# Two decoder layers on one core: the seven-product units of the down-projection reordered, with their sums in x's room, none in a layer's last pass, and the convolution released two pieces later

## The chip, the core and the metric

The kernel is one launch on one core of a Trainium2 chip. The metric is the device time of that launch in microseconds, lower is better. Three runs of the kernel before took 2187.38, 2190.59 and 2194.48 us, so the median is 2190.59 us.

## What is computed

Two layers on x of 256 tokens by 2048 features. Layer 0 is a mixer AB (gated spatial mixing and a gated linear recurrence), layer 1 a mixer C (forgetting attention with 16 heads). Each is followed by a gated MLP with a causal width-3 convolution, and this MLP is where the change is:

```python
D_MODEL, SEQ, FFN_HIDDEN = 2048, 256, 5632

def conv_ffn(h, w_up, conv_w, conv_b, w_down):
    z = h @ w_up                                   # 256 x 11264
    zp = jnp.pad(z, ((0, 0), (2, 0), (0, 0)))
    z = sum(conv_w[j] * zp[:, j:j + seq] for j in range(3)) + conv_b
    a, b = jnp.split(z, 2, axis=-1)
    return (jax.nn.silu(a) * b) @ w_down           # 256 x 2048

for l in range(2):
    x = x + mixer(rms_norm(x, mix_norm[l]))        # mixer_ab, then mixer_c
    x = x + conv_ffn(rms_norm(x, ffn_norm[l]), ...)
```

All of it is in float32, and the input is drawn from a seed.

## The kernel before

**Products in three parts.** A float32 factor is split into a high part and the rest, both in the matmul's own format, and every product is three matmuls (high by high, high by rest, rest by high). Activations are split once. Each weight tile is loaded by a DMA into a tile `w` (128 x 1024, 512 KB, pool of 5), `halves` (L185, L186) makes `wh` on ScalarE (a copy) and `wl` on VectorE (a subtraction), and TensorE takes `wh` and `wl`. The sets of `wh` and `wl` are few: three, and in the MLP two more for some of the turns.

**Pieces.** `project_four` (L381, L382 and L379) runs over pieces: one weight tile is two blocks of 128 in the contraction by 512 outputs, and gives 12 matmuls of 512 columns (2 halves of the tokens, 2 blocks, 3 parts), so one DMA of 512 KB, one split on ScalarE and one on VectorE stand beside 12 matmuls.

**The MLP.** `up(j0)` makes four tiles of 128 hidden features: two `four`s of 8 pieces, one for a and one for b. Each result goes from PSUM to `z` (ScalarE, L1421), is turned on VectorE (`STREAM_TRANSPOSE`, L482) and by 16 DMAs of 32 KB from `tmp` to `zt` (8 issued by SyncE, here SP, 8 by GpSimd, here POOL, L491). After a number of ticks (`LAG` = 6; a tick is about one piece) the convolution follows, one of four tiles per tick: ScalarE L1435, VectorE L1436 and L1437, then Silu on ScalarE for a; for b a product (L1459) and the split into `hid` (L499, L501). `down` multiplies `hid` with `w_down`. `STEPS` sets the order: three groups of `up`, each followed by a pass of `down` over 12 hidden tiles, and a last pass over 8 hidden tiles. A pass has four quarters q of 512 outputs; sums over passes are kept in `y`. In the last pass of a layer each quarter is turned back (`add_y`: L482, L491) and added to x (L1482). In layer 1 quarter 3 of the last pass is made feature by feature (`project`, L325), added (L1562) and written out.

**Seven products for eight.** The first two hidden tiles of a pass and two quarters of the outputs form a 2 x 2 by 2 x 2 block product, which `seven` makes with 7 products of 3 matmuls (L434 to L436) and sums of operands, for the 8 of plain pieces. Its weights are b1 and b2; VectorE makes four sums of 128 x 512 (L447 to L450), `parts` splits b1, b2, t (two sums) and half of t4, ScalarE copies two PSUM banks (L456, L460), VectorE adds two (L465, L470). The sums of activations are in `comb` (made by `combos`, L394 to L406). One unit is set into the pieces of the last `up` ahead of a pass (quarters 0 and 1), one into quarters 0 and 1 (for 2 and 3); for the last pass one unit stands in quarter 3 of the pass ahead. That is 7 units per layer, 14 in all. `t` lies in the room of x's tiles 8 to 11 and `comb` in that of 12 to 15; those two quarters of x wait in DRAM (`away`, L1518) and come back (`x_back`, L1527) in the layer's last pass. `t4` takes one of the two `zt` buffers. In L470 the copy of x0 has to be read before TensorE may add the last product to x0.

**Who sets the order.** Each engine and each DMA queue takes its instructions in the order in which the compiler's scheduler wrote them, by priority (program order) and by what its own model holds to be ready. `in_order` and `held` pin splits, sums and convolutions against each other on ScalarE and VectorE. SP issues the weight loads (L198, L443), half of the turning DMAs and x's return, in one queue.

Of the kernel before, what the change touches and what calls it, by code (L numbers as in the profile page):

```python
# [8 lines left out]
F32 = mybir.dt.float32  # L9
# [6 lines left out]
P = 128  # L16
# [8 lines left out]
BLK = 32  # L25
LAG = 6
FORGET = 4
PAIR = 5
# [27 lines left out]
def tile_trunk(ctx: ExitStack, tc: tile.TileContext, x, pp_d, cst_d, mlev_d, msk_d,  # L56
# [17 lines left out]
    xload = []  # L74
    for c0, n in ((0, 2), (2, 2), (4, 2), (6, 2), (8, 4), (12, 4)):
        t = cp.tile([P, n, S], F32, tag=f"x{c0}", name=f"x{c0}")
        xload.append((t, c0, n))
        xT += [t[:, i] for i in range(n)]
# [329 lines left out]
    def seven(w4s, a, comb, lo, banks4, sums, spare):  # L408
# [31 lines left out]

        b1, b2 = (wp.tile([P, 1024], F32, tag="w", name=nm("w"), bufs=5) for _ in range(2))
        for w, src in zip((b1, b2), sl):
            in_order("w", nc.sync.dma_start(w.rearrange("p (m c) -> p m c", m=4), src))  # L443
        yield
        tick()
        t, t4 = sums()
        then(V.tensor_tensor(block(t, 0), block(b2, 1), block(b2, 0), ALU.subtract))  # L447
        then(V.tensor_tensor(block(b2, 0), block(b2, 0), block(b1, 0), ALU.subtract))
        then(V.tensor_tensor(block(t, 1), block(t, 0), block(b1, 0), ALU.add))
        then(V.tensor_tensor(block(t4, 0), block(b1, 1), block(t, 1), ALU.subtract))  # L450
        yield
        (x1, x0), (x2, x3) = banks4()
        (a11h, a21h, a11l, a21l), (a12h, a22h, a12l, a22l) = ([left(t_, i) for i in range(4)] for t_ in a())
        first = parts(b1)
        product(x0, a11h, a11l, first, 0, True)
        SC.activation(x1, x0, AF.Copy)  # L456
        yield
        second = parts(b2)
        product(x3, *both(1), second, 0, True)
        SC.activation(spare, x3, AF.Copy)  # L460
        product(x1, a12h, a12l, first, 1)
        yield
        third = parts(t)
        product(x0, *both(2), third, 1)
        V.tensor_tensor(x2, x0, spare, ALU.add)  # L465
        yield
        tick()
        fourth = parts(t4, 0)
        product(x0, *both(0), third, 0)
        V.tensor_tensor(x3, x0, spare, ALU.add)  # L470
        yield
        product(x2, *both(3), second, 1)
        product(x0, a22h, a22l, fourth, 0)

# [923 lines left out]
    def ffn(l, norm, last):  # L1398
# [13 lines left out]
        def four(j0, inset=None):  # L1412
# [3 lines left out]
            def empty():  # L1416
                while norm.Rt is None:
                    yield
                z = [hp.tile([P, 512], F32, tag="z", name=nm("z"), bufs=2) for _ in range(2)]
                for T in range(2):  # L1420
                    SC.activation(cols4(z[T]), of_rows(ps[T]), AF.Copy, scale=norm.Rt[:, T:T + 1])  # L1421
                transposed(lambda T: z[T], tmp, zt)
                for _ in range(LAG):
                    yield
# [83 lines left out]
        comb, right = [None, None], [None]  # L1508
        away = [(t, c0, dp.tile([P, 4, S], F32, tag=f"xs{c0}", name=nm("xs"))) for t, c0, n in xload if n == 4]

        def combine(k):
            while len(hid) < k + 2:
                yield
            if k == 0:
                while not (norm.Rt is not None):
                    yield
                for _, c0, xs in away:
                    nc.gpsimd.dma_start(xs, part[c0][0])  # L1518
                right[0] = cp.tile([P, 1024], F32, tag="x8", name=nm("sums"))
            t = cp.tile([P, 1024], F32R, tag="x12", name=nm("comb"))  # L1520
# [11 lines left out]
        def begin(q, k0):  # L1532
# [6 lines left out]
            def sums():  # L1539
                while comb[0] != k0:  # L1540
                    tick()
                return right[0], hp.tile([P, 4, S], F32, tag="zt", name=nm("sums"), bufs=2).rearrange("p m t -> p (m t)")

# [4 lines left out]
        def down(k0, n, first, final, begun, after):  # L1548
            acts = hid[k0:k0 + n]
            if final and last:  # L1550
                x_back()
                add_y(3, False)
            for q in range(4):
                if last and final and q == 3:
# [9 lines left out]
                    return  # L1564
                if q == 0 and not final:
                    later, gen = begin(2, k0)
                    inset = (gen, max(0, n // 2 - 4), False)
                elif q == 1 and not final:
                    inset = (gen, 0, True)
                elif q == 3 and after:  # L1570
                    coming, gen = begin(0, k0 + n)
                    inset = (gen, 0, True)
                else:
                    inset = None
                if q < 2 or not final:
                    ps, ks = begun[q % 2], range(2, n, 2)
                else:
                    ps, ks = None, None
                ps = project_four(w_dn[l, 4 * q:4 * q + 4], acts, n, k0, ks=ks, ps=ps, inset=inset)
                if q == 1:  # L1580
                    if not final:
                        begun = later
                    if final and not last:
                        x_back()
                    elif not final:
                        queue.append(combine(k0 + n))
# [6 lines left out]
                if final:  # L1593
                    add_y(q, True)
            return coming if after else None

# [3 lines left out]
        for g, (now, ahead) in enumerate(STEPS):  # L1600
            while 4 * j0 < k0 + 4 * (now + ahead):
                inset = None
                if 4 * (j0 + 1) >= k0 + 4 * (now + ahead):
                    begun, gen = begin(0, k0)
                    inset = (gen, 1, True)
                up(4 * j0, inset)
                j0 += 1
            n, final = 4 * now, g == len(STEPS) - 1
            while len(hid) < k0 + n:
                tick()  # L1610
            begun = down(k0, n, g == 0, final, begun, g + 1 < len(STEPS) and 4 * j0 >= k0 + n + 4 * sum(STEPS[g + 1]))
            k0 += n
# [91 lines left out]
```

## Time and profile before

| what | value |
|---|---|
| median of 3 runs | 2190.59 us (2187.38 to 2194.48) |
| the profiled execution | 2195.88 us, span 2194.0 us |
| TensorE matmuls (PE) | 2165.7 us busy, 99% of the span |
| VectorE (DVE), ScalarE (ACT) | 1697.8 us (77%), 1341.9 us (61%) |
| GpSimd (POOL) | 476.4 us (22%) |
| moved by DMA | 487.80 MB, mean 222 GB/s |
| granted TensorE clock, mean | 0.998 |

A matmul's row says 0.38 us, but the next one starts 0.216 us after it: they overlap, and their ends are modelled. So the 99% do not tell how often TensorE stands still; the number of matmuls in a stretch of time does, against a stretch in which nothing is missing. "Idle before" names the time an engine stood before an instruction and what ended it. PEld is the load of the stationary operand; SPq is SP as a DMA queue.

### The profile page before, as it was taken

What the parts mean: (1) busy time and instruction counts of PE and PEld (TensorE: products, weight loads), DVE (VectorE), ACT (ScalarE), POOL (GpSimd) and SP (SyncE); (2) the same over time, 40 slices, a digit from 0 to 9 for tenths busy, and PEclk for the clock granted to TensorE, in tenths of its full rate; (3) what the DMA queues carried; (4) which work ended last, traced back from release to release, by engine and by line L of the source; (5) the groups of instructions that cost most, each with busy time, mean ns of one, the idle gap of its engine ahead of it and who ended that gap; (6) DMA issues with size and microseconds to landing.
All of it is one profiled execution on the core that took longest, in us unless ns stands there. A gap on an engine that the chain in (4) does not pass through costs nothing.

```text
span 2194.0 us, 32344 instructions
## 1 busy us (share of the span) xinstructions
PE 2165.7 (99%) x10694; PEld 1885.9 (86%) x10694; DVE 1697.8 (77%) x2481; ACT 1341.9 (61%) x1952; POOL 476.4 (22%) x869
## 2 busy tenths in 40 slices
PE   9999999999999999999999999999999999999998
PEld 8888888888888888878888888888888888888886
DVE  7888768878678866787887787878788578767786
ACT  6677766757566555664565566666566566455652
POOL 0352231221021011201233444221220021012102
PEclk9999999999999999999999999999999999999999
DMA  8755778786767767766777777778777676667766
GB/s 302 215 173 177 227 224 251 236 233 208 230 212 224 227 216 214 210 215 204 254 236 223 243 212 212 220 237 258 222 224 227 219 225 204 221 211 214 228 211 192
DMA packets 493480, 487.80 MB, mean 222 GB/s; under 512 B 115488, under 2 KB 460208, under 8 KB 493184
## 3 DMA queue, kind: packets, MB, share of 16 engines
q1 hardware_dynamic: 466464, 455.50, 66.4%
q0 software_dynamic: 25408, 28.08, 5.4%
q10 hardware_dynamic: 1440, 2.15, 0.3%
q8 instruction: 84, 1.38, 0.3%
q14 instruction: 84, 0.69, 0.1%
HBM read 437.34 MB, written 4.21 MB: 201 GB/s over the span
## 4 chain that ended last, share of the span: by engine, by line
PE 72%; DVE 11%; DMA 8%; SPq 4%; ACT 3%; issue 2%; POOL 0%; ACTq 0%; DVEq 0%
PE pm L381 11%; PE pm L382 11%; PE pm L379 11%; PE px L381 6%; PE px L382 6%; PE px L379 6%; PE pm L351 4%; PE pm L350 4%; PE pm L352 4%; DVE wl L186 4%; SPq L491 3%; DMA w<-in_w_dn 3%; DMA w<-in_w_up 3%; DMA zt<-tmp 1%; DVE conv L1436 1%
## 5 line engine op out<-in xcount | busy, mean ns | idle before, releaser
L186 DVE TENSOR_TENSOR wl<-w,wh 128x1024 fp32r<-128x1024 f32 (+1 forms) x820 | 985.0, 1219 | 360.1 <-ACT wh L185 352.4
L185 ACT ACTIVATE wh<-w 128x1024 fp32r<-128x1024 f32 (+1 forms) x820 | 850.3, 1049 | 540.5 <-PE pm L382 195.9
L491 POOL DMA_DIRECT2D zt<-tmp x413 | 223.6, 549 | 1141.0 <-DVE tmp L482 896.5
L381 PE MATMUL pm<-wl,a 128*128 128x512 f32 x1024 | 388.8, 380 | 2.2 <-DVE wl L186 2.2
L379 PE MATMUL pm<-wh,a 128*128 128x512 f32 x1024 | 388.6, 380 | 0.0
L382 PE MATMUL pm<-wh,a 128*128 128x512 f32 x1024 | 388.1, 379 | 0.0
L381 PE MATMUL px<-wl,a 128*128 128x512 f32 x704 | 267.6, 380 | 4.9 <-DVE wl L186 4.9
L379 PE MATMUL px<-wh,a 128*128 128x512 f32 x704 | 266.6, 379 | 1.6 <-ACT wh L185 1.6
L382 PE MATMUL px<-wh,a 128*128 128x512 f32 x704 | 266.8, 379 | 0.0
L381 PEld LDWEIGHTS pm<-wl,a 128*128 128x128 f32 x1024 | 193.5, 189 | 31.6 <-DVE wl L186 4.7
L379 PEld LDWEIGHTS pm<-wh,a 128*128 128x128 f32 x1024 | 193.4, 189 | 28.1 <-ACT wh L185 0.7
L382 PEld LDWEIGHTS pm<-wh,a 128*128 128x128 f32 x1024 | 193.5, 189 | 27.3
L350 PE MATMUL pm<-wh,a 128*128 128x512 f32 x416 | 158.9, 382 | 1.3 <-ACT wh L185 1.3
L351 PE MATMUL pm<-wl,a 128*128 128x512 f32 x416 | 158.6, 381 | 0.6 <-DVE wl L186 0.6
L352 PE MATMUL pm<-wh,a 128*128 128x512 f32 x416 | 158.4, 381 | 0.0
L381 PEld LDWEIGHTS px<-wl,a 128*128 128x128 f32 x704 | 133.0, 189 | 26.6 <-DVE wl L186 7.9
L379 PEld LDWEIGHTS px<-wh,a 128*128 128x128 f32 x704 | 132.8, 189 | 21.5 <-ACT wh L185 2.8
L382 PEld LDWEIGHTS px<-wh,a 128*128 128x128 f32 x704 | 133.1, 189 | 18.7
L1435 ACT ACTIVATE conv<-zt,pp 128x256 f32<-128x256 f32 x176 | 97.0, 590 | 84.4 <-DMA zt<-tmp 57.7
L1436 DVE SCALAR_TENSOR_TENSOR conv<-zt,pp,conv 128x255 f32<-128x255 f32 x176 | 81.5, 481 | 64.8 <-ACT conv L1435 54.4
L491 POOL DMA_DIRECT2D turn<-tmp x159 | 86.4, 551 | 200.3 <-DVE tmp L482 161.3
L379 PE MATMUL px<-wh,hid 128*128 128x512 f32 x296 | 112.2, 382 | 4.3 <-ACT wh L185 4.3
(320 smaller groups left out, 3500.6 us busy)
## 6 DMA issues: line engine op xcount, KB each, us to landing
w<-in_w_up SPq DMA_DIRECT2D x352, 512.0 KB, 5.1
w<-in_w_dn SPq DMA_DIRECT2D x176, 512.0 KB, 5.0
w<-in_w_cqkv SPq DMA_DIRECT2D x96, 512.0 KB, 5.0
w<-in_w_abo SPq DMA_DIRECT2D x32, 512.0 KB, 5.0
w<-in_w_cg SPq DMA_DIRECT2D x32, 512.0 KB, 5.0
w<-in_w_co SPq DMA_DIRECT2D x32, 512.0 KB, 4.8
zt<-tmp SPq DMA_DIRECT2D x416, 32.0 KB, 2.6
zt<-tmp POOLq DMA_DIRECT2D x413, 32.0 KB, 2.6
```

The lines of the kernel that those rows point to most:

```text
L185: r = deep["wh"] = SC.activation(wh, w, AF.Copy)
L186: deep["wl"] = V.tensor_tensor(wl, w, wh.bitcast(F32), ALU.subtract)
L350: PE.matmul(to_two(ps[T]), ah, h, start=k + i == 0, stop=False)
L351: PE.matmul(to_two(ps[T]), ah, l, start=False, stop=False)
L352: deep["last"] = PE.matmul(to_two(ps[T]), al, h, start=False, stop=k + i == KT - 1)
L379: PE.matmul(to_rows(ps[T]), ah, h, start=not begun and k + i == ks[0], stop=False, skip_group_check=loose)
L381: PE.matmul(to_rows(ps[T]), ah, l, start=False, stop=False, skip_group_check=loose)
L382: deep["mm"] = deep["last"] = PE.matmul(to_rows(ps[T]), al, h, start=False, stop=not more and k + i == ks[-1] + 1, skip_group_check=loose)
L491: queues[(a + b) % len(queues)].dma_start(dst[BLK * b:BLK * (b + 1), :, a * n:(a + 1) * n], tmp[BLK * a:BLK * (a + 1), b * 4 * n:(b + 1) * ...
L1435: held(SC.activation(c, z, AF.Identity, bias=pp[:, cb:cb + 1], scale=w(2)))
L1436: V.scalar_tensor_tensor(c[:, 1:], z[:, :S - 1], w(1), c[:, 1:], ALU.mult, ALU.add)
```

## The change

`seven` takes its sums in another order and in other rooms: b2 is loaded straight into x's room (tile x0), and the sums `near` and `far` go to the rooms of x4 and x8, so a unit ties one `w` tile and no `zt` buffer. Its parts come in the order b1, near, far, half of b2, so that a part is used up soon after it is made, and the last two products stand one piece behind the product that L470 reads. x has four tiles of four feature blocks each; all four go to DRAM at the start of an MLP and come back in quarter 1 of the pass ahead of the last one. The last pass of a layer has no unit (12 in all), and the unit in `up` starts at piece 2 where it was piece 1. The convolution is released 8 ticks behind, where it was 6.

```diff
+LATE = 8
-    for c0, n in ((0, 2), (2, 2), (4, 2), (6, 2), (8, 4), (12, 4)):
+    for c0, n in ((0, 4), (4, 4), (8, 4), (12, 4)):
...
-        b1, b2 = (wp.tile([P, 1024], F32, tag="w", name=nm("w"), bufs=5) for _ in range(2))
+        b1 = wp.tile([P, 1024], F32, tag="w", name=nm("w"), bufs=5)
+        b2, near, far = sums()
...
-        t, t4 = sums()
-        then(V.tensor_tensor(block(t, 0), block(b2, 1), block(b2, 0), ALU.subtract))
-        then(V.tensor_tensor(block(b2, 0), block(b2, 0), block(b1, 0), ALU.subtract))
-        then(V.tensor_tensor(block(t, 1), block(t, 0), block(b1, 0), ALU.add))
-        then(V.tensor_tensor(block(t4, 0), block(b1, 1), block(t, 1), ALU.subtract))
+        then(V.tensor_tensor(block(near, 0), block(b2, 0), block(b1, 0), ALU.subtract))
+        then(V.tensor_tensor(block(far, 0), block(b2, 1), block(b2, 0), ALU.subtract))
+        then(V.tensor_tensor(block(near, 1), block(far, 0), block(b1, 0), ALU.add))
+        then(V.tensor_tensor(block(far, 1), block(b1, 1), block(near, 1), ALU.subtract))
...
-        first = parts(b1)
-        product(x0, a11h, a11l, first, 0, True)
+        t = parts(b1)
+        product(x0, a11h, a11l, t, 0, True)
         SC.activation(x1, x0, AF.Copy)
+        first = t
         yield
-        second = parts(b2)
-        product(x3, *both(1), second, 0, True)
+        t = parts(near)
+        product(x3, *both(1), t, 0, True)
         SC.activation(spare, x3, AF.Copy)
         product(x1, a12h, a12l, first, 1)
-        yield
-        third = parts(t)
-        product(x0, *both(2), third, 1)
+        product(x0, *both(2), t, 1)
         V.tensor_tensor(x2, x0, spare, ALU.add)
         yield
         tick()
-        fourth = parts(t4, 0)
-        product(x0, *both(0), third, 0)
+        t = parts(far)
+        product(x0, *both(0), t, 0)
         V.tensor_tensor(x3, x0, spare, ALU.add)
         yield
-        product(x2, *both(3), second, 1)
-        product(x0, a22h, a22l, fourth, 0)
+        last = parts(b2, 1)
+        product(x2, *both(3), last, 1)
+        product(x0, a22h, a22l, t, 1)
...
-                for _ in range(LAG):
+                for _ in range(LATE):
...
-        away = [... for t, c0, n in xload if n == 4]
+        away = [... for t, c0, n in xload]
-                right[0] = cp.tile([P, 1024], F32, tag="x8", name=nm("sums"))
+                right[:] = [cp.tile([P, 1024], F32, tag=f"x{c0}", name=nm("sums")) for c0 in (0, 4, 8)]
...
             if final and last:
-                x_back()
                 add_y(3, False)
-                elif q == 3 and after:
-                    coming, gen = begin(0, k0 + n)
-                    inset = (gen, 0, True)
+                if q == 1 and not final:
+                    begun = later
+                    if after:
+                        x_back()
...
-                    inset = (gen, 1, True)
+                    inset = (gen, 2, True)
```

**Where the order moves, first place: TensorE at the end of the unit set into layer 0's third group of `up`.** `hid` and `comb` rows are the unit's products, `a` rows are pieces of `up`. Before:

```order
L434 MATMUL px_9169<-wh_9232,comb_7562 128x512
L435 MATMUL px_9169<-wl_9233,comb_7562 128x512
L436 MATMUL px_9169<-wh_9232,comb_7562 128x512
L434 MATMUL pm_9170<-wh_9198,comb_7562 128x512
L435 MATMUL pm_9170<-wl_9199,comb_7562 128x512
L436 MATMUL pm_9170<-wh_9198,comb_7562 128x512
L434 MATMUL px_9169<-wh_9268,hid_7429 128x512
L435 MATMUL px_9169<-wl_9269,hid_7429 128x512
L379 MATMUL px_9095<-wh_9282,a_4047 128x512
L379 MATMUL px_9096<-wh_9282,a_4047 128x512
L436 MATMUL px_9169<-wh_9268,hid_7429 128x512
```

Now:

```order
L383 MATMUL px_9076<-wh_9262,a_4047 128x512
L380 MATMUL px_9076<-wh_9262,a_4051 128x512
L382 MATMUL px_9076<-wl_9263,a_4051 128x512
L383 MATMUL px_9076<-wh_9262,a_4051 128x512
L435 MATMUL pm_9182<-wh_9279,comb_7558 128x512
L436 MATMUL pm_9182<-wl_9280,comb_7558 128x512
L437 MATMUL pm_9182<-wh_9279,comb_7558 128x512
L435 MATMUL px_9181<-wh_9248,hid_7455 128x512
L436 MATMUL px_9181<-wl_9249,hid_7455 128x512
L437 MATMUL px_9181<-wh_9248,hid_7455 128x512
L380 MATMUL px_9075<-wh_9295,a_4073 128x512
```

Before, three matmuls stand between the product into px_9169 that L470 reads and the next one into the same bank. Now that product (into px_9181, not in these rows) stands ahead of the whole piece wh_9262, of which the first rows here are the end, so 15 matmuls are between.

**The same place on VectorE.** L465 and L470 are the unit's two adds, L186 (now L187) the splits, L1436 and L1437 (now L1437 and L1438) the convolution. Before:

```order
L465 TENSOR_TENSOR pm_9170<-px_9169,p_1579_8895 128x512
L1436 SCALAR_TENSOR_TENSOR conv_9276<-zt_9072,pp,conv_9276 128x255
L1437 SCALAR_TENSOR_TENSOR conv_9276<-zt_9072,pp,conv_9276 128x254
L470 TENSOR_TENSOR pm_9171<-px_9169,p_1579_8895 128x512
L186 TENSOR_TENSOR wl_9283<-w_9281,wh_9282 128x1024
L186 TENSOR_TENSOR wl_9307<-w_9305,wh_9306 128x1024
```

Now:

```order
L465 TENSOR_TENSOR pm_9182<-px_9181,p_1573_8881 128x512
L187 TENSOR_TENSOR wl_9280<-sums_4593,wh_9279 128x4x128
L1437 SCALAR_TENSOR_TENSOR conv_9289<-zt_9052,pp,conv_9289 128x255
L187 TENSOR_TENSOR wl_9296<-w_9294,wh_9295 128x1024
L1438 SCALAR_TENSOR_TENSOR conv_9289<-zt_9052,pp,conv_9289 128x254
L470 TENSOR_TENSOR pm_9183<-px_9181,p_1573_8881 128x512
```

The split of the piece that follows the unit (wl_9283 before, wl_9296 now) stood behind L470 and now stands ahead of it.

**Second place: ScalarE behind the first `four` of layer 0's second group.** z is the result leaving PSUM, the wh rows are splits, conv the first step of the convolution. Before:

```order
L1421 ACTIVATE z_6241<-pm_6093,Rt_4186 128x512
L185 ACTIVATE wh_6337<-w_6336 128x1024
L185 ACTIVATE wh_6360<-w_6359 128x1024
L185 ACTIVATE wh_6383<-w_6382 128x1024
L185 ACTIVATE wh_6406<-w_6405 128x1024
L1435 ACTIVATE conv_6354<-zt_6239,pp 128x256
L1435 ACTIVATE conv_6377<-zt_6239,pp 128x256
L1435 ACTIVATE conv_6400<-zt_6239,pp 128x256
L1435 ACTIVATE conv_6449<-zt_6239,pp 128x256
```

Now:

```order
L1422 ACTIVATE z_6241<-pm_6093,Rt_4186 128x512
L186 ACTIVATE wh_6337<-w_6336 128x1024
L186 ACTIVATE wh_6355<-w_6354 128x1024
L186 ACTIVATE wh_6373<-w_6372 128x1024
L186 ACTIVATE wh_6396<-w_6395 128x1024
L1436 ACTIVATE conv_6390<-zt_6239,pp 128x256
L1436 ACTIVATE conv_6439<-zt_6239,pp 128x256
L186 ACTIVATE wh_6445<-w_6444 128x1024
L98 ACTIVATE conv_6390<-conv_6390 128x256
```

The first of the four still stands behind four splits; the third and the fourth, which stood right behind it, now have splits ahead of them.

**Third place: SP in layer 1's last pass.** x<-xs is x's return, zt<-tmp the turning DMAs, w the weight loads. Before:

```order
L198 DMA w_20706<-in_w_dn 128x4x256
L1527 DMA x_20568<-xs_14656 128x1024
L491 DMA zt_20571<-tmp_20570 32x4x64 x9
L198 DMA w_20748<-in_w_dn 128x4x256
L198 DMA w_20766<-in_w_dn 128x4x256
L491 DMA zt_20647<-tmp_20646 32x4x64 x8
L198 DMA w_20784<-in_w_dn 128x4x256
L491 DMA zt_20727<-tmp_20726 32x4x64 x8
L198 DMA w_20803<-in_w_dn 128x4x256
```

Now:

```order
L199 DMA w_20692<-in_w_dn 128x4x256
L199 DMA w_20710<-in_w_dn 128x4x256
L492 DMA zt_20475<-tmp_20474 32x4x64 x9
L199 DMA w_20729<-in_w_dn 128x4x256
L199 DMA w_20748<-in_w_dn 128x4x256
L199 DMA w_20790<-in_w_dn 128x1024
L492 DMA zt_20571<-tmp_20570 32x4x64 x8
L199 DMA w_20822<-in_w_dn 128x1024
L199 DMA w_20856<-in_w_dn 128x1024
L199 DMA w_20895<-in_w_dn 128x1024
```

Before, eight weight loads stood behind the first nine turning DMAs; now six do, all of them ahead of the third set of turning DMAs, and x's return is no longer in this pass.

More of the change, by code (lines that the diff above doesn't have):

```diff
@@ L1508, in ffn @@
         comb, right = [None, None], [None]
-        away = [(t, c0, dp.tile([P, 4, S], F32, tag=f"xs{c0}", name=nm("xs"))) for t, c0, n in xload if n == 4]
+        away = [(t, c0, dp.tile([P, 4, S], F32, tag=f"xs{c0}", name=nm("xs"))) for t, c0, n in xload]
         def combine(k):
@@ L1541, in sums @@
                     tick()
-                return right[0], hp.tile([P, 4, S], F32, tag="zt", name=nm("sums"), bufs=2).rearrange("p m t -> p (m t)")
+                return right
             spare = hp.tile([P, 512], F32, tag="z", name=nm("p5"), bufs=2)
@@ L1564, in down @@
                     return
[L1565 to L1568, printed above, removed]
-                    inset = (gen, 0, True)
-                elif q == 3 and after:
-                    coming, gen = begin(0, k0 + n)
[L1572 to L1575, printed above, removed]
-                    ps, ks = begun[q % 2], range(2, n, 2)
-                else:
-                    ps, ks = None, None
+                inset = ps = ks = None
+                if not final:
+                    ps, ks = begun[q % 2], range(2, n, 2)
+                    if q == 0:
+                        later, gen = begin(2, k0)
+                        inset = (gen, 2, False)
+                    elif q == 1:
+                        inset = (gen, 0, True)
                 ps = project_four(w_dn[l, 4 * q:4 * q + 4], acts, n, k0, ks=ks, ps=ps, inset=inset)
[L1580 to L1583, printed above, removed]
+                if q == 1 and not final:
+                    begun = later
+                    if after:
                         x_back()
-                    elif not final:
+                    else:
                         queue.append(combine(k0 + n))
@@ L1594, in down @@
                     add_y(q, True)
-            return coming if after else None
         j0, k0, hid = 0, 0, []
@@ L1610, in ffn @@
                 tick()
-            begun = down(k0, n, g == 0, final, begun, g + 1 < len(STEPS) and 4 * j0 >= k0 + n + 4 * sum(STEPS[g + 1]))
+            down(k0, n, g == 0, final, begun, g == len(STEPS) - 2)
             k0 += n
```

## The prediction

> **What bounds the kernel now.** I read the page first (TensorE 99% busy), then the busy times by stretch, because a pipelined matmul looks busy while it waits. The columns are the stretch in us, its length, then busy us and number of instructions of TensorE, its weight loads, VectorE, ScalarE and GpSimd, the granted clock, the DMA engines' share and GB/s.
>
> ```profile
> 550.00:700.00 150.00, 149.56 (x693) 130.35 (x692) 104.94 (x133) 88.04 (x111) 21.64 (x40) 1.00 0.71 223
> 700.00:750.00 50.00, 48.48 (x221) 41.15 (x220) 44.21 (x66) 33.06 (x47) 4.33 (x8) 1.00 0.69 214
> 750.00:900.00 150.00, 150.00 (x696) 131.35 (x695) 100.45 (x129) 82.14 (x107) 21.69 (x40) 1.00 0.71 217
> 900.00:950.00 50.00, 45.00 (x203) 37.53 (x202) 38.56 (x55) 31.74 (x44) 8.66 (x16) 1.00 0.73 219
> 950.00:1050.00 100.00, 98.90 (x454) 85.16 (x453) 85.20 (x121) 53.94 (x72) 17.30 (x32) 1.00 0.69 211
> 1600.00:1700.00 100.00, 98.05 (x449) 84.11 (x448) 84.64 (x120) 64.23 (x90) 17.31 (x32) 1.00 0.77 232
> 1850.00:1900.00 50.00, 47.93 (x219) 40.72 (x218) 41.97 (x59) 29.38 (x36) 4.33 (x8) 1.00 0.69 214
> 2050.00:2150.00 100.00, 97.43 (x443) 82.76 (x442) 86.29 (x119) 59.60 (x77) 12.46 (x23) 1.00 0.67 208
> ```
>
> 750 to 900 us is the yardstick: 696 matmuls of 512 columns in 150 us, one each 0.2155 us, nothing missing. Against that rate the others lack 3, 11, 29 and 10 matmuls in layer 0 and 15, 13 and 21 in layer 1: 102, or 22 us. This is the MLPs' standing time, and all of these stretches hold seven-product units. Everything else is matmuls that the change does not remove. What TensorE waited for there:
>
> ```profile
> PE px L381 <- DVE wl L186: 6.1, 9, 2.7
> PE px L379 <- ACT wh L185: 5.9, 4, 4.3
> PE pm L381 <- DVE wl L186: 4.3, 8, 1.2
> PE px L434 <- DVE pm L470: 1.9, 4, 1.2
> PE pm L434 <- DVE px L470: 1.5, 4, 0.7
> ```
>
> So it waits for splits, and for L470 itself. One unit's end in order of time shows how the two hang together:
>
> ```profile
> 738.84 0.38 PE L436 MATMUL px<-wh,comb 128*128 128x512 f32 x1
> 739.12 0.69 DVE L470 TENSOR_TENSOR px<-pm,p 128x512 f32<-128x512 f32 x1
> ...
> 739.96 0.45 PE L434 MATMUL pm<-wh,hid 128*128 128x512 f32 x1 [0.74 <-DVE px L470]
> ...
> 740.65 2.36 DVE L186 TENSOR_TENSOR wl<-w,wh 128x1024 fp32r<-128x1024 f32 x2 [0.51 <-ACT wh L185]
> ...
> 741.93 0.48 PE L381 MATMUL pm<-wl,hid 128*128 128x512 f32 x1 [0.56 <-DVE wl L186]
> ```
>
> The last product waits for L470, and the next piece's split stands behind L470 in VectorE's queue, so TensorE waits a second time. After each unit the splits' lead over TensorE is nil, and anything late then is paid in full.
>
> **The change, part by part.** Durations (x times, busy us, mean ns, idle before):
>
> ```profile
> L186 DVE TENSOR_TENSOR wl<-w,wh 128x1024 fp32r<-128x1024 f32 x812 | 979.7, 1224 | 356.5 <-ACT wh L185 348.9 <-DMA zt<-tmp 4.0
> L450 DVE TENSOR_TENSOR sums<-w,sums 128x512 f32<-128x512 f32 x14 | 9.5, 675 | 0.3
> L470 DVE TENSOR_TENSOR px<-pm,p 128x512 f32<-128x512 f32 x7 | 4.9, 696 | 2.4 <-PE pm L436 2.4
> ```
>
> *Two units fewer.* A unit is 21 matmuls for 24, so one unit less per layer is 2 x 3 x 0.2155 = 1.3 us more on TensorE, all on the path. VectorE loses four sums, two adds and 3.5 splits per unit and gains two splits: 4 x 0.675 + 2 x 0.70 + 1.5 x 1.22, some 6 us per layer off an engine that idles 350 us. That is worth nothing in itself; what counts is that two units' ends go.
>
> *The unit's order.* At a unit's end three matmuls (0.65 us) cover L470 today, and it needs its 0.70 us and the way there and back. Now 15 matmuls (3.2 us) cover it, and the split of the next piece stands ahead of it (first place). So both waits of the timeline should go at the 12 units that remain. Parts used at once also free their `wh` and `wl` a piece or two sooner, and b1 alone holds a `w` tile where b1 and b2 did, so the splits can run one piece (2.6 us) further ahead. I count 12 of the 22 us to this. The ends: 2.6 us, if only the two dropped units' ends go (0.74 + 0.56 us each), and 22 us, if every stall in these stretches was of this kind. I take 12 because the two waits cost about 1 us at each of 14 units, a bit more than half of 22; the rest, 900 to 950 us above all, falls differently in the two layers (29 lacking there, and 21 in the twice as long stretch that holds the same place of layer 1), so the order does not fix it.
>
> *Eight pieces behind.* ScalarE and VectorE do stand still for the convolution:
>
> ```profile
> ACT conv L1435 <- DMA zt<-tmp: 57.7, 21, 6.7
> DVE conv L1436 <- ACT conv L1435: 54.4, 21, 6.1
> ```
>
> But the order (second place) has the first convolution behind the same four splits as before; only the third and fourth of each set yield to a split. I take nothing for it, with -4 to +4 us: a split one place earlier at 44 sets is a gain where the lead is nil, and the convolutions that now lie two pieces later fall on the second unit of each pass.
>
> *x in DRAM.* Eight 512 KB transfers more, one half on POOL's queue at the start of an MLP, one half on SP's between weight loads (size and median us from issue to landing):
>
> ```profile
> w<-in_w_dn SPq DMA_DIRECT2D x176, 512.0 KB, 5.0
> x<-xs SPq DMA_DIRECT2D x4, 512.0 KB, 4.6
> ```
>
> The DMA engines are 0.69 to 0.77 busy in the stretches above, so they fit; behind the POOL issues stand turning DMAs, behind the SP issues weight loads. On SP the return of the `comb` room waits for the unit's last `comb` matmul, with five pieces (13 us) already issued; a load lands in 5.0 us and its two splits take about 2.5 (twice the 1.22), so some 5 us are to spare. I take 1 us for all of it, between 0 and 6. The b2 loads wait on SP for the unit before to finish with that room, three pieces back, when five `w` tiles are as far ahead as SP can be anyway: nothing.
>
> *The last pass.* In layer 1 SP feeds it like this:
>
> ```profile
> 2144.56 6.05 SPq L491 DMA_DIRECT2D zt<-tmp  x9
> 2150.73 1.07 SPq L198 DMA_DIRECT2D w<-in_w_dn  x2
> 2155.03 5.12 SPq L491 DMA_DIRECT2D zt<-tmp  x8
> 2160.26 0.53 SPq L198 DMA_DIRECT2D w<-in_w_dn  x1
> 2162.94 5.10 SPq L491 DMA_DIRECT2D zt<-tmp  x8
> 2168.08 2.09 SPq L198 DMA_DIRECT2D w<-in_w_dn  x4
> ```
>
> Three loads in 24 us, where a piece is eaten each 2.6 us; and so:
>
> ```profile
> 2173.40 1.12 PE L379 MATMUL px<-wh,hid 128*128 128x512 f32 x2 [4.28 <-ACT wh L185]
> ...
> 2175.68 0.63 PE L379 MATMUL px<-wh,hid 128*128 128x512 f32 x1
> ```
>
> 4.28 us of standing, then 3.4 us in which a matmul takes 0.63 us for 0.38 and follows the last at half the rate, 1.7 us more: 6 us. With x's return gone from this pass and six loads for eight behind the turning DMAs, the loads of pieces 11 to 16 are issued while TensorE is near piece 4 to 6, and the stall goes. What is late next is the last quarter's turn, sums and write, which hang on quarter 2's end and so come forward with it. I take 5 us, between 0 and 6.
>
> The half rate also follows a shorter stall, at the start of mixer C, which the change leaves as it is:
>
> ```profile
> 1066.16 0.70 PE L350 MATMUL pm<-wh,a 128*128 128x512 f32 x2 [1.27 <-ACT wh L185]
> ...
> 1067.90 0.63 PE L352 MATMUL pm<-wh,a 128*128 128x512 f32 x1
> ```
>
> [...]
>
> **The sum.** Against the profiled execution's own 2195.88 us (span 2194.0): +1.3 - 12 + 0 + 1 - 5 = -14.7, so 2181.2 us. That execution lies 5.3 us over the median of the runs, 2190.59 us. Part of the 5.3 must be stalls which the median run does not have, but the 12 us counts only what the order fixes in every run, so I keep the difference: 2190.6 - 14.7 = 2176 us.
>
> **Rivals.**
> *The stalls only move.* The convolution's wait for its turning DMAs (57.7 us on ScalarE) is what empties the lead, and its place is unchanged; then "eight behind" does not do what it says, the unit's next wait takes the place of L470's, and only the last pass and the two dropped units' ends are gained: 1.3 + 1 - 2.6 - 5 = -5.3, so 2185 us. For it: the worst stretch, 900 to 950 us. Against it: the stretch 750 to 900 us has the same convolutions, no unit's products, and lacks nothing.
> *Transfers share the engines.* [...] As a mechanism here: x's eight more transfers push the weight loads back one for one, 512 KB at 217 GB/s or 2.4 us each, 19 us in all, against 1.3 - 12 - 5 = -15.7: 2194 us. Against it: the share of 0.71, and the four transfers of before, behind which the stretches show no lack of their own.
> *x's room holds up SP (slower).* Weight loads stand in SP's queue behind eight issues that wait for a unit to finish: x's return once per layer, and b2 of the second unit of three passes per layer. Should each empty the lead as the last pass does now, that is 8 x 6 = 48 us, against the same 15.7 us gained: some 2223 us. It decides from the third such stall on. For it: SP's gaps above, made by just such issues. Against it: five pieces issued ahead in the order.
>
> **How the numbers follow.** Forecast 0.74, the stalls only move 0.14, shared engines 0.05, SP held up 0.07. About 0.3% (6.6 us) is what a measurement of this kernel can tell from no change, so faster means below 2184.0 and slower above 2197.2. Forecast is faster, 0.74; the second and third cases are same, 0.19; the fourth is slower, 0.07. The range: at the low end all 22 us, the whole 6 us of the last pass and nothing for x, 2190.6 + 1.3 - 22 - 6 = 2164; at the high end the first rival's 2185 and the 5 us that x's transfers may cost beyond the 1 taken, 2190. That leaves out the last two rivals and some runs past both ends.
>
> **What would show it.** Right: no wait of TensorE's L435 for the add (3.4 us before); each stretch of an MLP near 4.64 matmuls per us; no gap of 4 us and no half rate in the last pass; 6 matmuls more. The convolution's wait on ScalarE stays near 50 us. Wrong: the stretches with units still lack 80 or more matmuls; or TensorE stands 3 us or longer within five pieces behind x's return; or SP's waits at the b2 loads are long and followed by late splits.

## The result, and the profile after

The kernel after takes 2164.3 us (median; 2161.98 to 2165.80), the kernel before 2190.27 us on the same chip: ratio 0.9879, 95% interval 0.9860 to 0.9898. The gain is 26.0 us where 14.7 was forecast, and the median lies at the very low end of the range (2164). The profiled execution takes 2161.98 us (span 2160.2), 33.9 us less than that of before, and has 10,700 matmuls, six more.

The busy times by stretch, with the columns of the prediction:

```profile
550.00:700.00 150.00, 150.00 (x697) 131.35 (x696) 106.32 (x137) 88.63 (x112) 21.64 (x40) 1.00 0.75 232
...
900.00:950.00 50.00, 48.90 (x226) 42.03 (x224) 39.99 (x58) 32.58 (x45) 10.89 (x21) 1.00 0.74 227
950.00:1050.00 100.00, 99.57 (x460) 86.75 (x461) 82.34 (x118) 52.83 (x72) 17.73 (x33) 1.00 0.73 224
1050.00:1100.00 50.00, 50.00 (x263) 42.77 (x262) 46.38 (x88) 30.43 (x51) 10.32 (x19) 1.00 0.81 270
1600.00:1700.00 100.00, 100.00 (x466) 87.55 (x465) 79.42 (x109) 62.91 (x83) 12.99 (x24) 1.00 0.73 227
...
2050.00:2150.00 100.00, 100.00 (x485) 88.11 (x484) 80.37 (x107) 49.26 (x56) 18.57 (x35) 1.00 0.75 233
```

At 4.64 matmuls per us, 50 us hold 232 and 100 us 464. Layer 1 lacks nothing any more (its last stretch holds short matmuls of the last pass too, and so more than 464). Layer 0 lacks 6 at 900 to 950 us and 4 behind that. What TensorE still waited for in the whole span (us, times, longest):

```profile
PE px L435 <- DVE pm L465: 1.0, 1, 1.0
PE pm L382 <- DVE wl L187: 1.0, 3, 0.4
...
PE px L382 <- DVE wl L187: 0.2, 1, 0.2
```

A unit's end, at nearly the same time as the one shown of before:

```profile
732.36 0.38 PE L437 MATMUL pm<-wh,comb 128*128 128x512 f32 x1
...
733.62 0.69 DVE L470 TENSOR_TENSOR px<-pm,p 128x512 f32<-128x512 f32 x1
...
735.17 0.38 PE L435 MATMUL px<-wh,comb 128*128 128x512 f32 x1
...
735.82 0.38 PE L435 MATMUL pm<-wh,hid 128*128 128x512 f32 x1
```

L437 ends the product that L470 reads, and L470 ends at 734.31. The first of the two last products starts at 735.17, and the second, which writes the bank that L470 has read, at 735.82, both with no wait in their rows. The one wait for an add that is left in the list (1.0 us) is for the unit's first add, L465. And SP in the last pass of layer 1:

```profile
2089.95 23.27 SPq L199 DMA_DIRECT2D w<-in_w_dn  x12
2117.02 5.77 SPq L492 DMA_DIRECT2D zt<-tmp  x9
2122.89 2.15 SPq L199 DMA_DIRECT2D w<-in_w_dn  x3
2127.38 5.12 SPq L492 DMA_DIRECT2D zt<-tmp  x8
2132.55 1.54 SPq L199 DMA_DIRECT2D w<-in_w_dn  x3
```

Three weight loads stand between two sets of turning DMAs, where one or two stood, and twelve are out ahead of the first set.

Where the 33.9 us of the two profiled executions lie: I summed, from both traces, by how much each matmul of 512 columns started later than 0.216 us behind one of the same size. These are called late starts below.

| where | before, us | after, us |
|---|---|---|
| layer 0, MLP, from 500 us on | 12.8 | 2.5 |
| start of mixer C (1050 to 1100 us) | 4.4 | 0.1 |
| layer 1, MLP, up to 2150 us | 11.6 | 0.0 |
| last pass, from 2150 us on | 6.8 | 0.0 |

All four together are 33.0 us less after than before. The start of mixer C is one that the prediction left as it was. The convolution's wait on ScalarE stands nearly where it stood (57.7 us before), that on VectorE is some 10 us shorter (54.4 before):

```profile
ACT conv L1436 <- DMA zt<-tmp: 54.9, 23, 5.4
...
DVE conv L1437 <- ACT conv L1436: 44.8, 17, 5.1
```

### The profile page after: what moved, and what is told of

It reads as the page before. It is cut to its first block, busy times and chain, and to the rows that moved or that the text cites. A ratio compares the mean times of both kernels' runs of the same rounds, so it can differ in the third digit from the quotient of the medians.

```text
span 2160.2 us, 32319 instructions
## 1 busy us (share of the span) xinstructions
PE 2152.4 (100%) x10700; PEld 1887.7 (87%) x10700; DVE 1683.7 (78%) x2451; ACT 1338.6 (62%) x1942; POOL 476.6 (22%) x873
## 4 chain that ended last, share of the span: by engine, by line
PE 94%; DVE 2%; DMA 1%; SPq 1%; ACT 1%; issue 1%; DVEq 0%; ACTq 0%
PE pm L382 15%; PE pm L380 15%; PE pm L383 15%; PE px L380 10%; PE px L382 10%; PE px L383 10%; PE pm L351 5%; PE pm L352 4%; PE pm L353 4%; PE pm L237 1%; PE pm L316 1%; SPq L492 1%; DVE wl L187 1%; PE pm L319 1%; PE pm L326 0%
## 5 line engine op out<-in xcount | busy, mean ns | idle before, releaser
L187 DVE TENSOR_TENSOR wl<-w,wh 128x1024 fp32r<-128x1024 f32 (+1 forms) x808 | 974.9, 1216 | 354.5 <-ACT wh L186 345.5
L186 ACT ACTIVATE wh<-w 128x1024 fp32r<-128x1024 f32 (+1 forms) x808 | 842.1, 1049 | 515.3 <-PE pm L383 206.2
L383 PEld LDWEIGHTS px<-wh,a 128*128 128x128 f32 x704 | 133.1, 189 | 18.9
L380 PEld LDWEIGHTS px<-wh,a 128*128 128x128 f32 x704 | 133.1, 189 | 18.9
L382 PEld LDWEIGHTS px<-wl,a 128*128 128x128 f32 x704 | 133.1, 189 | 18.9
L1436 ACT ACTIVATE conv<-zt,pp 128x256 f32<-128x256 f32 x176 | 100.1, 589 | 71.8 <-DMA zt<-tmp 54.9
L1437 DVE SCALAR_TENSOR_TENSOR conv<-zt,pp,conv 128x255 f32<-128x255 f32 x176 | 83.1, 479 | 53.2 <-ACT conv L1436 44.8
L382 PE MATMUL px<-wl,hid 128*128 128x512 f32 x304 | 115.3, 379 | 0.2 <-DVE wl L187 0.2
```

What stands on the lines that cost most here:

```text
L186: r = deep["wh"] = SC.activation(wh, w, AF.Copy)
L187: deep["wl"] = V.tensor_tensor(wl, w, wh.bitcast(F32), ALU.subtract)
L380: PE.matmul(to_rows(ps[T]), ah, h, start=not begun and k + i == ks[0], stop=False, skip_group_check=loose)
L382: PE.matmul(to_rows(ps[T]), ah, l, start=False, stop=False, skip_group_check=loose)
L383: deep["mm"] = deep["last"] = PE.matmul(to_rows(ps[T]), al, h, start=False, stop=not more and k + i == ks[-1] + 1, skip_group_check=loose)
L1436: held(SC.activation(c, z, AF.Identity, bias=pp[:, cb:cb + 1], scale=w(2)))
```

## The experiments

Each kernel is the one before or the one after with one part changed. Gains are medians less the kernel before on the same chip; the kernel after stands at -26.0 by that count (-26.2 when it was run again), and by their 95% intervals such gains are uncertain by 2 to 4 us either way.

### The unit's order

**The order alone, in the kernel before** (14 units, a lag of 6, rooms as before).

```diff
...
-        third = parts(t)
-        product(x0, *both(2), third, 1)
+        product(x0, *both(2), t, 1)
...
-        product(x2, *both(3), second, 1)
-        product(x0, a22h, a22l, fourth, 0)
+        last = parts(b2, 1)
+        product(x2, *both(3), last, 1)
+        product(x0, a22h, a22l, t, 1)
```

> The kernel before with the unit's new order alone (near, far, half of b2; the last two products a piece behind the far product); b2 stays in a w tile, near in x8's room, far in a zt buffer, 14 units, LAG 6. If the order is what ends the standing time, the stretches with units stop lacking matmuls and of the 26 us between the two kernels some 15 to 18 are here: about 2173 us. If it is the rooms (two w tiles and a zt buffer tied by a unit), or the convolution's two pieces, about 2187 us, with the two waits at a unit's end gone and others in their place. If it is the last pass, about 2188 us.

2186.75 us, ratio 0.9971 (0.9960 to 0.9981): -6.5 us. TensorE's waits in that run:

```profile
PE px L381 <- DVE wl L186: 7.0, 8, 3.0
PE pm L381 <- DVE wl L186: 3.3, 6, 1.1
PE px L379 <- ACT wh L185: 3.2, 1, 3.2
PE px L434 <- DVE pm L464: 2.6, 2, 1.6
PE pm L434 <- DVE px L464: 2.1, 2, 1.1
```

The wait for L470 is gone from the list, but 4.7 us of the same products wait for the unit's first add (L464 here, L465 before) instead, and 13.5 us of waits for splits are left, of 16.3 before. So the order removes the wait that it was said to remove, and gives the splits back little of their lead.

**All but the order and the rooms:** the kernel before, without the last pass's unit and with a lag of 8. (It also lacks x's further transfers, and its unit in `up` starts at piece 1.)

> The kernel before with no unit in the last pass and the convolution 8 ticks behind: the changed kernel without the unit's new order and rooms. If the three parts add up (order 6.5, last pass 14, convolution 9, measured each alone), about 2170 us; if the order is worth only what the joined end (3 us) and the rooms (1 us) lose, 2167 to 2168 us; if my prediction's 12 us for the order holds in this company, 2176 us.

2172.84 us, 0.9915 (0.9900 to 0.9931): -19.0, so the order and its rooms, with those two, are worth 7.0 us on top of the rest. Its list shows them, 4.0 us at the unit's products and, with a smaller row, 2.8 at splits:

```profile
PE pm L434 <- DVE px L470: 2.0, 3, 1.1
PE px L434 <- DVE pm L470: 2.0, 3, 1.1
PE px L381 <- DVE wl L186: 1.8, 2, 1.6
```

**The end joined:** the kernel after without the pause that sets the last two products a piece further back.

```diff
-        yield
         last = parts(b2, 1)
```

> The changed kernel with the last two products put back right behind the far product (no piece between), all else as changed. If TensorE's wait for the second add and the split behind it are the cost, it comes back as about 1 us at each of 12 units: about 2175 us, and L435 waits for L470 again. If the lead is kept by the parts and rooms, the wait is covered: 2164 to 2167 us.

2167.47 us, 0.9881 (0.9868 to 0.9895): -25.8. By the difference nothing, by the medians 3 us; the wait for L470 comes back in four places, 2.0 us in all. It can't be told from no change.

**The rooms undone:** b2 in a `w` tile and `far` in a `zt` buffer, order as after.

```diff
-        b1 = wp.tile([P, 1024], F32, tag="w", name=nm("w"), bufs=5)
-        b2, near, far = sums()
+        b1, b2 = (wp.tile([P, 1024], F32, tag="w", name=nm("w"), bufs=5) for _ in range(2))
...
+        near, far = sums()
...
-                return right
+                return right[0], hp.tile([P, 4, S], F32, tag="zt", name=nm("sums"), bufs=2).rearrange("p m t -> p (m t)")
```

> The changed kernel with b2 back in a w tile and far in a zt buffer; order, last pass and convolution as changed. If the order carries the gain, 2164 to 2168 us. If the rooms do (one w tile less for the loads, a zt buffer less for the turning DMAs), 2175 us or more, with ScalarE waiting for weight loads around the units.

2165.22 us, 0.9873 (0.9860 to 0.9887): -28.0. The rooms in x's tiles bring nothing that these runs can tell.

### The convolution's lag

**A lag of 8 alone, in the kernel before.**

```diff
-                for _ in range(LAG):
+                for _ in range(LAG + 2):
```

> The kernel before with the convolution released 8 ticks behind, all else as before. By the prediction 2190 us, within 4. If the run of convolutions ahead of the splits is a cost of its own, some 6 to 10 us less than before, so about 2184 us, the waits at units' ends smaller but still there (three matmuls cover the second add). If it helps only together with the new order, 2190 us.

2183.33 us, 0.9957 (0.9944 to 0.9971): -9.3.

**A lag of 6 in the kernel after** (`LATE = 6`).

> The changed kernel with the convolution released 6 ticks behind again, all else as changed. My prediction gave the 8 nothing, since the first convolution's place is the same; then 2164 to 2167 us. The order alone (6 us) and the last pass alone (14 us) leave some 6 to 8 us of the 26 to 28 unexplained and the rooms bring none of it; if the 8 ticks bring them, because the other convolutions of a set no longer stand in one run ahead of the splits on VectorE, about 2173 us, with the waits of the order-alone run back (TensorE for the first add, then for the split behind it).

2176.97 us, 0.9929 (0.9917 to 0.9942): -15.6, so 10.4 us of the gain are lost. The edit to which the prediction gave nothing is worth 9 to 10 us, by both runs. (Between the run without the last pass's unit, shown below at -13.9, and the one with the old order, -19.0, it is 5.1.) By what? A lag can shorten the convolution's wait for its turning DMAs, or spread the work that stands between two splits. The kernel with a lag of 6 has both the longer wait

```profile
ACT conv L1436 <- DMA zt<-tmp: 79.3, 29, 5.7
```

and more convolutions in a row: I counted, in the MLPs of each trace (500 to 1050 us, and from 1540 us on), the stretches of VectorE between one split and the next that hold two convolutions or more. There are 53 before and 25 with a lag of 8 alone; 28 after and 55 with the lag of 6, in 12 of which four stand in one row. The length of a stretch alone does not tell: 7 of them hold over 5 us of other work after, and 8 with the lag of 6. The next run tries to part the wait from the row.

**The first of a set at 6 again, the others spread behind it.**

```diff
-                    yield
+                    for _ in range(1 if i else 3):
+                        yield
```

with `LATE = 6`, and the same in the loop for b, which puts the four convolutions at ticks 6, 9, 10 and 11.

> The changed kernel with the first convolution of each set released at tick 6 and the others at 9, 10 and 11, as the 8 ticks have them. If the worth of the 8 (12.7 us when undone) lies in the other three no longer standing in one run with the first, ahead of the splits, 2164 to 2168 us. If it lies in the first coming later, 2174 to 2177 us.

2162.87 us, 0.9865 (0.9848 to 0.9881): -28.9; nothing is lost. The wait is up again, by 7.7 us, and the count of stretches is 28, as after.

```profile
ACT conv L1436 <- DMA zt<-tmp: 62.6, 22, 5.7
```

**Lags of 10 and of 12.**

> The changed kernel with the convolution released 10 ticks behind. If ScalarE's wait for the turning DMAs (55 us) is worth something to TensorE, it falls and a few of the 9 us of standing that are left go: 2160 to 2163 us. If the wait is covered as the splits' lead is now, 2164 us. If the convolution then runs into the next set's, whose buffers it holds, 2168 us or more.

> The kernel after with the convolution 12 pieces behind and not 8. If a longer lag goes on spreading the convolutions among the splits and its gain has not ended at 10 (2160.5 us), 2157 to 2160 us. If the gain ends where the stretches of other work between two splits are already short, 2160 to 2163 us. If the tiles that hold the pieces' sums come to be waited for, over 2165 us.

10: 2160.47 us, 0.9855 (0.9840 to 0.9870), -31.3. 12: 2162.15 us, 0.9869 (0.9855 to 0.9883), -28.3, beside the kernel after on the same chip:

> The kernel after, unchanged, so that it stands on the same chip beside the two others: 2162 to 2166 us by either theory.

2164.23 us, 0.9879 (0.9863 to 0.9895). With 10 the wait on ScalarE is nearly gone, with 12 there is none in the list:

```profile
ACT conv L1436 <- DMA zt<-tmp: 7.9, 4, 2.8
```

Some 47 us of waiting less than at 8 brought some 4 to 5 us, and the last 8 us brought none. The counts (6 and 12 such stretches, 28 at 8) fall and rise as the times do. So the spread goes with the gains and most likely carries most of them; a share of the wait is not excluded, since with the first at 6 it is 62.6 us and not the 79.3 of the plain lag of 6. A lag of 10 beats both kernels: none of its runs (up to 2161.16) is as slow as the fastest of the kernel after (2161.98, and 2163.26 when it was run again).

### The last pass

**Before, without the last pass's unit**, and x's return in the pass ahead of it.

```diff
             if final and last:
-                x_back()
                 add_y(3, False)
...
-                elif q == 3 and after:
-                    coming, gen = begin(0, k0 + n)
-                    inset = (gen, 0, True)
...
-                    if final and not last:
+                    if after:
                         x_back()
```

> The kernel before with no unit in a layer's last pass and x's return in the pass ahead, all else as before. The last pass's stall (4.3 us and 1.7 us at half rate) goes, two units' ends go, 1.3 us are added: about 2184 us by my sum. If the last pass also carries the wait at the start of mixer C (some 4 us, which I had left as it is), about 2180 us. If the unit's order carries nearly everything, 2188 us or more.

2179.36 us, 0.9937 (0.9924 to 0.9951): -13.9. That is the case in which the last pass also carries the wait at the start of mixer C: against before, the late starts from 1000 to 1100 us fall from 5.3 to 0.1 us, those from 2050 to 2150 us from 4.7 to 1.4, and those behind that from 6.8 to nothing. Less 1.3 us for the matmuls added, these make about the gain.

**After, with both put back:** the unit in the last pass, and x's return (four tiles in each layer) in that pass.

> The changed kernel with the unit of the last pass back (14 units, x's return in the last pass as before), order, rooms and convolution as changed. It saves 6 matmuls, 1.3 us: 2163 us if the new order covers the last pass too. If the last pass suffers from x's return and the loads queued behind the turning DMAs, whatever the unit's order, the stall near the end and the wait at the start of mixer C come back, 10 to 12 us: about 2175 us.

2181.24 us, 0.9947 (0.9934 to 0.9959): -11.3, so 14.9 us are lost. The profiled span is 19.6 us longer than that of the kernel after, and by the sum of late starts all of it lies in the last passes and right behind: 5.9 us from 1000 to 1100 us and 13.7 from 2050 us on. The stretch of mixer C's start, and SP in layer 1's last pass:

```profile
1050.00:1100.00 50.00, 47.56 (x242) 39.70 (x241) 43.78 (x84) 29.96 (x49) 9.52 (x18) 0.97 0.79 263
```

```profile
2094.69 9.15 SPq L199 DMA_DIRECT2D w<-in_w_dn  x6
2111.97 0.34 SPq L1528 DMA_DIRECT2D x<-xs  x1
2114.56 0.92 SPq L199 DMA_DIRECT2D w<-in_w_dn  x2
2117.10 0.34 SPq L1528 DMA_DIRECT2D x<-xs  x1
2121.86 0.37 SPq L199 DMA_DIRECT2D w<-in_w_dn  x1
2122.46 0.34 SPq L1528 DMA_DIRECT2D x<-xs  x1
2122.84 0.98 SPq L199 DMA_DIRECT2D w<-in_w_dn  x2
2126.40 0.34 SPq L1528 DMA_DIRECT2D x<-xs  x1
2128.30 6.47 SPq L492 DMA_DIRECT2D zt<-tmp  x9
```

Five loads in the 16 us from the first x<-xs to the turning DMAs (2128.30), where TensorE, at 12 matmuls of 0.216 us or 2.6 us a piece, eats six. What SP waited for at x's return in this stretch:

```profile
SPq L1528 <- DVE wl L187: 9.8, 3, 8.0
...
SPq L1528 <- PE px L437: 2.5, 1, 2.5
```

These are the rooms that the unit holds: its last split, and its last matmul.

**x's return late, but no unit in the last pass.**

```diff
+                x_back()
...
+                if q == 1 and final and not last:
+                    x_back()
...
-                    if after:
-                        x_back()
-                    else:
+                    if not after:
```

> The changed kernel (12 units) with x's return alone back in the last pass, as before (quarter 1 in layer 0, the pass's start in layer 1). The run with 14 units lost 17 us, all of it in the last pass and at the start of mixer C. If x's return in SP's queue is the cause, 2175 us or more, with the stall near the end; if it is the unit, whose loads, sums and splits stand in front of the pass, 2164 to 2168 us.

2163.96 us, 0.9870 (0.9855 to 0.9885): -27.9. The return by itself costs nothing that can be told in that place.

**The unit and the return put back, but the return issued by GpSimd.**

```diff
-                nc.sync.dma_start(t, xs)
+                nc.gpsimd.dma_start(t, xs)
...
```

> The kernel after with the unit of the last pass and x's return in that pass put back (as in the run with fourteen units, 2181.2 us, 17 above the kernel after), but x's return is issued by GpSimd's queue and not by SyncE's. If the 17 us come from SyncE standing at x's return while it waits for the unit's rooms, with the weights' loads queued behind, they go: 2161 to 2167 us, and no wait of over 2 us by ScalarE on the down projection's weights in the last pass. If they come from the unit itself, its splits and sums taking VectorE's and ScalarE's time at the end, they stay: 2177 to 2184 us.

2171.52 us, 0.9912 (0.9898 to 0.9927): -18.9. Neither end of what was expected: of the 14.9 us, 7.6 come back with another issuer, 7.3 stay. The standing moves to GpSimd, behind which no weight loads queue:

```profile
POOL x L1528 <- DVE wl L187: 95.3, 6, 38.5
```

The late starts at mixer C and from 2050 to 2150 us are gone (0.8 and 0.0 us). What is left is one place at the end of layer 1, TensorE and, behind it, ScalarE and SP:

```profile
2150.47 1.23 PE L326 MATMUL pm<-hid,wh 128*128 128x256 f32 x4 [4.33 <-ACT wh L186]
...
2152.32 1.06 PE L326 MATMUL pm<-hid,wh 128*128 128x256 f32 x4
...
2155.91 0.61 PE L326 MATMUL pm<-hid,wh 128*128 128x256 f32 x4
```

```profile
2149.36 1.06 ACT L186 ACTIVATE wh<-w 128x1024 fp32r<-128x1024 f32 x1 [7.29 <-DMA w<-in_w_dn]
```

```profile
2121.50 6.73 SPq L492 DMA_DIRECT2D zt<-tmp  x9
2128.27 1.97 SPq L199 DMA_DIRECT2D w<-in_w_dn  x2
2132.04 5.10 SPq L492 DMA_DIRECT2D zt<-tmp  x8
2137.19 0.59 SPq L199 DMA_DIRECT2D w<-in_w_dn  x1
2140.19 5.12 SPq L492 DMA_DIRECT2D zt<-tmp  x8
2145.36 2.02 SPq L199 DMA_DIRECT2D w<-in_w_dn  x4
```

That is the picture of the kernel before: three loads in 24 us, a stall of 4.3 us, and half the rate behind it (four matmuls of 256 columns take 1.06 us, then 0.61), some 2.8 us more: 4.33 + 2.8 = 7.1 of the 7.3. So the 5 us of the prediction were this stall, and the other half was SP standing at x's return. That the unit's loads are what leaves only three loads between the turning DMAs is read from SP's order; no run tried it by itself.

### x through DRAM

**x saved twice and fetched twice**, 16 transfers of 512 KB more than in the kernel after.

```diff
+                    nc.gpsimd.dma_start(xt, part[c0][0])
...
+                nc.sync.dma_start(t, xt)
```

> The changed kernel with x saved twice (to two places in DRAM) and fetched twice (the second over the first): 16 transfers of 512 KB more, the result unchanged. If transfers beside the weights cost one for one, 2.4 us each: about 2200 us. If the share of the DMA engines leaves room, 2164 to 2167 us; if SP's queue is held up at the return, a stall within five pieces behind it, 2168 to 2176 us.

2168.24 us, 0.9886 (0.9873 to 0.9900): -24.3, so 2 to 4 us for 16, some 0.1 to 0.25 us each, which is hardly more than such a gain is uncertain by.

## Why the prediction was right or wrong, step by step

Its sign and its first mechanism hold; the sum was short by 11.3 us, and three steps of it failed. That the range reaches down to the time measured is luck: its low end takes all 22 us of the MLPs for the order, which brought some 7, and 6 us for the last pass, which brought 14.

- *Two units fewer*, +1.3: the six matmuls are there. Their price is not told apart from the rest of the last pass.
- *The unit's order*, -12: mis-sized. It is worth 6.5 us alone and 7.0 put back. The prediction read 22 us in the MLPs rightly (24.4 us of late starts in the traces, 2.5 after), but gave more than half of them to the wait at L470 and the wait behind it, about 1 us at each of 14 units. Its own rows have that wait at eight units (4 and 4): in the trace of before these are 4.7 us of late starts at L470 and 3.4 us right behind, 8.1 in all. With the new order alone 13.5 us of waits for splits stay. "The order does not fix it" was said of the stretch from 900 to 950 us alone; it holds for most of the 22.
- *The x rooms.* "So the splits can run one piece (2.6 us) further ahead" was counted in with the order. Undoing the rooms loses nothing that can be told.
- *Eight pieces behind*, 0 with -4 to +4: **this step failed.** The gain is 9 to 10 us by itself in either kernel. The prediction looked at which split the first convolution stands behind, found it unmoved, and stopped; the same rows of the order showed that the third and fourth have a split ahead of them now, and that, by the counts and the run with the first at 6, was most of the gain. It named it, "a gain where the lead is nil", and capped it at 4.
- *x in DRAM*, +1 between 0 and 6: right. 16 transfers more cost 2 to 4 us, so eight are estimated at some 1 to 2.
- *The last pass*, -5 between 0 and 6: **this step failed.** It was worth 14 to 15 us with the two units' matmuls set against it. The stall at 2173 us that it priced is there (6.8 us of late starts, with the half rate: the granted clock is 0.52 from 2173.4 to 2176.8 us), but it was one of three places: 3.3 us more lay between 2050 and 2150 us, and 5.2 at the end of layer 0. x's return stood on SP, waiting for the unit's rooms, in each layer's last pass (9.8 us over the four issues of before); in the kernel with both put back, which returns four tiles per layer where before returned two, 7.6 us went when GpSimd issued it.
- *The start of mixer C*, "which the change leaves as it is": **this step failed.** The row at 1066.16, 1.27 us of waiting and the half rate behind it (a granted clock of 0.52 from 1067.5 to 1071.0 us), was the far end of the same queue in layer 0: SP issues mixer C's first weights behind x's return and the turning DMAs. Ahead of the last nine of these it had issued five of mixer C's loads before, four with both put back, and six after, without the last unit, and with GpSimd's return. The wait is gone after and wherever the unit is out of the last pass, and down to 0.8 us of late starts where the unit is back and GpSimd issues the return.
- *The difference to the median* was kept, rightly in part: the two profiled executions differ by 33.9 us, the medians by 26.0.

Of the rivals, *the stalls only move* was right in what it said of the convolution's wait (57.7 us, now 54.9) and wrong in what it made of it: the wait is not, in the main, what empties the lead. The run with the first convolution at 6 has 62.6 us of it and loses nothing, and the runs at 10 and 12 are almost rid of it and gain 2 to 5 us. What empties it, as far as the runs tell, is several convolutions one after the other between two splits. *Transfers share the engines* asked for 2.4 us a transfer, a price that no run shows; by the run with x saved and fetched twice it is some 0.1 to 0.25. *x's room holds up SP* had the mechanism, in the wrong place: returns that wait for a unit's rooms in a last pass did cost TensorE (7.6 us for eight), which is what the change takes away; in the kernel after they stand in the pass ahead of it, for 2.8 us at most, and no stall follows them. At the six b2 loads for which it took the same, and the working above took nothing, SP did stand:

```profile
SPq L445 <- DVE conv L1437: 54.2, 6, 10.4
```

Yet TensorE's longest wait for a split after is 0.4 us, and undoing the rooms gains nothing that can be told: this standing was covered.

Each alone in the kernel before, the order gives 6.5 us, the lag 9.3 and the last pass 13.9, 29.7 in all, less 1 to 2 for x's transfers, against the 26.0 measured. They are not quite independent: lag and last pass together give 19.0 where one by one they give 23.2. Differences uncertain by 2 to 4 us each leave open how much of that is real.

## What to carry to other kernels

An engine that feeds another in order lost its lead here, as far as the runs tell, where several pieces of other work stood in a row between two feeding instructions (53 such stretches before, 25 with a lag of 8 alone), so read the order for such rows, not only for who waits: a lag that left the first convolution behind the same splits was worth 9 to 10 us, and 47 us of waiting taken away, with most of the rows that were left, were worth 4 to 5. A DMA that waited for a room (up to 8.0 us, x's return with both put back) held up the loads behind it in its queue here, and the loads ahead decided whether it cost anything; when a stall near the end of a stage is priced, follow that queue back to the first issue that stood, and forward to the next stage, since the same issue was paid there too. Where the time of a stage is bounded by what a trace lacks against a full rate, let the range of each edit reach to all of that, also of an edit that seems to move nothing.

## What the runs showed of the hardware

- The half rate followed short waits here. With the fourteen units put back, mixer C starts like this:

```profile
1054.09 0.70 PE L351 MATMUL pm<-wh,a 128*128 128x512 f32 x2 [1.88 <-ACT wh L186]
1055.35 0.48 PE L352 MATMUL pm<-wl,a 128*128 128x512 f32 x1 [0.56 <-DVE wl L187]
...
1056.12 0.63 PE L352 MATMUL pm<-wl,a 128*128 128x512 f32 x1
...
1058.67 0.63 PE L353 MATMUL pm<-wh,a 128*128 128x512 f32 x1
```

  Waits of 1.88 and 0.56 us, and some 3.4 us of half rate: from 1056.1 to 1059.5 us the matmuls start 0.43 us apart, before the first wait and from 1059.9 us on 0.22 us; the mean granted clock from 1050 to 1100 us is 0.97. In the kernel before it followed waits of 1.27 and 0.59 us (the row at 1066.16 and the next one). Not each such wait had it: behind one of 2.72 us, which ended at 929.42 us in the kernel before, the matmuls start 0.22 us apart, with a granted clock of 1.00 from 929.4 to 933.0 us. What sets these cases apart was not shown. The waits of 1.88 and 0.56 us cost some 1.7 us more in what follows them, an estimate from 3.4 us at half the rate.
- The queue from which x's return is issued was worth 7.6 us for eight transfers, whose own issue takes some 0.34 us each on SP. What cost time with the fourteen units put back was not the issue but the standing ahead of it (up to 8.0 us in one row), and the loads queued behind stood with it: from 2103.8 to 2114.6 us SP issued none.
